# Trunk encoder with a mixture of experts on one core: 2 KB runs for the experts' first weights, norm vectors loaded ahead of weights, the first expert interleaved, and the embedding's second half added on GpSimd

## The chip, the cores and the metric

The kernel runs on 1 core of a Trainium2 chip. The metric is device time in microseconds (us) of one launch, the median of several runs. Engines: PE is TensorE's matmuls, PEld its weight loads, DVE is VectorE, ACT is ScalarE, POOL is GpSimd, SP is SyncE, which here only issues DMAs. All arithmetic is fp32 to the outside; TensorE multiplies in a rounded fp32 format, so that a product is made of three matmuls (below).

## The reference, cut to what matters

Two layers over 512 tokens of width 1024. In each, three mixers read one projection, an output projection follows, then a layer norm (LN1), a mixture of experts beside a gated embedding (PLE), and a second layer norm (LN2).

```python
for i in range(DEPTH):                                   # 2 layers
    u = h @ w_in[i]
    mix = concatenate([hyena(u), diff_attention(u), pool(u)]) @ w_out[i]
    h = layer_norm(DN_ALPHA * h + mix, ln1_g[i], ln1_b[i])          # LN1
    y_moe = hier_moe(h, ...)         # 1 of 4 groups, 2 of its 4 experts, per token
    y_ple = sigmoid(h @ ple_wg[i] + ple_bg[i]) * (p[i] @ ple_wp[i])
    h = layer_norm(DN_ALPHA * h + y_moe + y_ple, ln2_g[i], ln2_b[i])  # LN2

# one expert e of 16, of width 256, on the tokens sent to it:
y_e = (silu(x @ w1[e]) * (x @ w3[e]) * gate) @ w2[e]     # w1, w3: 1024x256, w2: 256x1024
```

## The kernel before, in words

The 512 tokens are four tiles t of 128 rows, `h[t]`, [128, 1024]. **Products.** Every fp32 operand is split into a rounded part and a rest, `whi` by ACT (L224) and `wlo` by DVE (L225); `mm3` then issues three matmuls, hi by hi (L218), hi by lo (L219), lo by hi (L220). Weights thus pass through four stations: a DMA into a slot `raw` issued from SP (L240), the cast, the subtraction, the matmuls.

**Units.** The work with weights is cut into units of up to 512 KB (`add`). `pump` issues loads ahead of use, as far as `ahead_raw` allows and slots of a pool of 34 of 4 KB per partition (`s4`) are free, and the splits as far as `ahead_split` allows; `fill(n)`, `fill_us` and `fill_to` emit the next units' matmuls. So the order of loads is the order of units, and a load waits, on SP's queue, until an older occupant of its slot is done with.

**LN1 and routing.** The layer emits w_out's product (`mo`, summed into h by DVE, L997), and each tile's norm as soon as its four sums are there: `moments` (L362, L364), `rsqrt` on POOL (L305, L308), `ln` (L334 `(h - mean) * gain`, L336 `* rstd + bias`), then its transposes into `hT` (L376). The tiles `gain` (two, 4 KB a partition each) and `bg`, the PLE's bias, are 512 KB DMAs each, broadcast to all partitions. They are issued from SP after `fill_to(i, "last")` under `P_LN`, hence behind the loads that this `fill_to` prefetches. Then come the routing logits `lgT`, `lg`, and a branch on overflow (L1351), which ends a stretch that the scheduler may reorder.

**Experts.** `add_expert_in` makes four units q for expert e: 256 rows of w1 and w3, two DMAs of 256 KB, "(k p) n -> p k n", so that a partition gets from each matrix two rows of 256 numbers (1 KB), 128 rows apart. The moving operand is then [128, 512], w1's and w3's columns side by side; the stationary one is a 128-column piece of `xT`. `gather` fetches an expert's tokens (`xe`), `expert_x` transposes them (`transpose_hl`, `tr`, L376) and splits them into `xT`; `expert_act` (L1293) makes silu and product, and transposes the result (L1298) into `actT`; `add_expert_out` multiplies by w2 into `ye`, which is scattered by a DMA that accumulates in DRAM (`yd`, L1263). `xe` of the next experts is gathered one or two ahead. Expert 0's first products are followed by its `expert_act` at once; from expert 1 on, units of the next stand between.

**PLE and tail.** `add_ple` computes the embedding's halves c = 0 and 1; c = 0 goes to `plz` tiles in `s4` slots, and from there accumulates into `yd` (L1234, POOL queue), c = 1 stays as `z1[t]`. After the last scatter SP loads `h` from `yd` (L1418). `tail_sum` adds for each tile the last two experts' rows (`el`, four matmuls a half, L1441) and z1. For a tile in `ZPE` (tile 1 in layer 0; 1, 2, 3 in layer 1) z1 and h are added on PE by an identity (L1438, L1445) and ACT writes h (L1446); for the others DVE adds the rows to z1 (L1449) and that to h (L1450). LN2 follows (L348, L350).

## Time and profile before

| what | value |
|---|---|
| time, median of 3 | 1038.74 us (1034.38 to 1038.75) |
| profiled execution: its own time | 1037.3 us |
| profiled execution: span, mean granted clock | 1035.5 us, 0.985 |
| busy: PE, PEld, DVE, ACT, POOL | 94%, 77%, 75%, 59%, 16% of the span |
| weights of the experts, 256 loads of 256 KB | 1 KB a run |
| expert stage, layers 0 and 1 | about 334 to 523 and 826 to 1011 us |

The times in the rows are microseconds from the span's start. A matmul's duration is longer than the step from one start to the next, since matmuls are pipelined; its step is read from the chain or from two starts.

### The profile page before, as it was taken

Reading aid. Unit: us, or ns where it says so; the run is one execution under the profiler, and the core shown is the slowest. Engines: PE = TensorE matmul, PEld = TensorE weight load, DVE = VectorE, ACT = ScalarE, POOL = GpSimd, SP = SyncE. Lnnn points to the kernel's source line nnn. Section 1 sums busy time; section 2 is a strip of 40 time slices with the busy share of each in tenths; the row PEclk is TensorE's granted clock in tenths of the full one; section 3 lists DMA queues with packets and bytes.
Section 4 is the critical chain, followed back from the end, with each engine's and each line's share of the span. In section 5 each row is a group of like instructions: output and inputs, shape, how many; then the busy total and the mean of one; then the engine's idle time right before and its main releaser. Section 6 shows DMA issues by size and latency. Waiting matters only on the chain. (4 is left out here: it accounts for less than half of the span.)

```text
span 1035.5 us, 14416 instructions
## 1 busy us (share of the span) xinstructions
PE 969.3 (94%) x4877; PEld 801.8 (77%) x4878; DVE 781.4 (75%) x1305; ACT 613.7 (59%) x1046; POOL 163.6 (16%) x158
## 2 busy tenths in 40 slices
PE   4999999999989999999989999999998999999896
PEld 3887888898867788777768889899776778877673
DVE  7576897777676788887984678847578587888795
ACT  5425464556653768886843336655645286888573
POOL 2101000000121223332112000000003122243111
PEclk9999999999999999999999999999999999999999
DMA  8816121221963999999975321222187399999963
GB/s 267 239 36 143 52 72 53 72 82 63 322 234 106 302 299 318 306 284 307 292 246 137 88 70 53 62 71 72 62 300 248 83 318 294 325 295 306 311 203 156
DMA packets 154922, 195.39 MB, mean 189 GB/s; under 512 B 20232, under 2 KB 123722, under 8 KB 154837
## 3 DMA queue, kind: packets, MB, share of 16 engines
q1 hardware_dynamic: 136405, 159.78, 46.6%
q0 software_dynamic: 18432, 34.57, 13.0%
q8 instruction: 42, 0.69, 0.3%
q14 instruction: 43, 0.35, 0.1%
HBM read 182.85 MB, written 27.26 MB: 203 GB/s over the span
## 5 line engine op out<-in xcount | busy, mean ns | idle before, releaser
L225 DVE TENSOR_TENSOR wlo<-raw,whi 128x1024 fp32r<-128x1024 f32 (+2 forms) x278 | 323.7, 1182 | 62.1 <-ACT whi L224 59.6
L224 ACT CAST whi<-raw 128x1024 fp32r<-128x1024 f32 (+2 forms) x278 | 277.1, 1024 | 24.4 <-DMA raw<-in_ple_wg_dram 6.4
L218 PE MATMUL e<-whi,xT 128*128 128x512 f32 x256 | 106.5, 416 | 2.7 <-ACT xT L224 1.7
L219 PE MATMUL e<-wlo,xT 128*128 128x512 f32 x256 | 103.5, 404 | 0.1
L220 PE MATMUL e<-whi,xT 128*128 128x512 f32 x256 | 101.7, 397 | 0.0
L218 PE MATMUL pj<-whi,hT 128*128 128x384 f32 x256 | 90.1, 353 | 2.3 <-ACT hT L224 1.8
L219 PE MATMUL pj<-wlo,hT 128*128 128x384 f32 x256 | 88.2, 345 | 0.3 <-DVE wlo L225 0.3
L220 PE MATMUL pj<-whi,hT 128*128 128x384 f32 x256 | 87.3, 342 | 0.1
L1263 POOL DMA_INDIRECT yd<-ye,rt_tok x28 | 53.5, 1910 | 202.6 <-ACT actT L224 122.0
L868 ACT ACTIVATE prob<-sc,mx 128x512 f32<-128x512 f32 x64 | 43.8, 688 | 40.4 <-DVE mx L867 38.0
L1257 POOL DMA_INDIRECT xe<-hd,rt_tok x32 | 48.8, 1525 | 90.1 <-PE tr L376 45.6
L308 POOL TENSOR_TENSOR ors<-rs_y,mhalf 128x4 f32<-128x4 f32 x8 | 8.5, 1056 | 336.7 <-DVE rs_y L307 336.7
L218 PEld LDWEIGHTS e<-whi,xT 128*128 128x128 f32 x256 | 48.8, 191 | 12.8 <-ACT xT L224 2.2
L219 PEld LDWEIGHTS e<-wlo,xT 128*128 128x128 f32 x256 | 48.8, 190 | 10.9 <-DVE wlo L225 2.4
L220 PEld LDWEIGHTS e<-whi,xT 128*128 128x128 f32 x256 | 48.7, 190 | 10.1
L218 PE MATMUL mo<-whi,YT 128*128 128x512 f32 x128 | 53.6, 419 | 0.0
L219 PE MATMUL e<-wlo,actT 128*128 128x512 f32 x128 | 51.2, 400 | 2.4 <-DVE wlo L225 2.4
L218 PEld LDWEIGHTS pj<-whi,hT 128*128 128x128 f32 x256 | 49.1, 192 | 4.8 <-ACT hT L224 2.5
L218 PE MATMUL pl<-whi,hT 128*128 128x512 f32 x128 | 50.8, 402 | 1.3 <-ACT whi L224 1.3
L219 PE MATMUL pl<-wlo,hT 128*128 128x512 f32 x128 | 51.4, 402 | 0.5 <-DVE wlo L225 0.5
L218 PE MATMUL e<-whi,actT 128*128 128x512 f32 x128 | 48.2, 398 | 3.8 <-ACT whi L224 2.9
L218 PE MATMUL pj<-hT,whi 128*128 128x512 f32 x128 | 51.1, 403 | 0.0
(344 smaller groups left out, 2310.7 us busy)
## 6 DMA issues: line engine op xcount, KB each, us to landing
raw<-in_moe_w_dram SPq DMA_DIRECT2D x256, 256.0 KB
raw<-in_moe_w_dram SPq DMA_DIRECT2D x64, 512.0 KB
raw<-in_w_in_dram SPq DMA_DIRECT2D x96, 128.0 KB
raw<-in_w_in_dram SPq DMA_DIRECT2D x16, 512.0 KB
raw<-in_ple_wg_dram SPq DMA_DIRECT2D x16, 512.0 KB
raw<-in_w_out_dram SPq DMA_DIRECT2D x14, 512.0 KB
tabi<-c_tabi_dram POOLq DMA_DIRECT2D x8, 516.0 KB, 4.9
tabf<-c_tabf_dram POOLq DMA_DIRECT2D x8, 512.0 KB, 5.6
```

Source lines behind the costliest of these rows:

```text
L218: mm(ps, a[0], b[0], start=start, stop=False)
L219: mm(ps, a[0], b[1], start=False, stop=False)
L220: mm(ps, a[1], b[0], start=False, stop=stop)
L224: self.nc.scalar.copy(hi, src)
L225: self.nc.vector.tensor_sub(lo, src, hi.bitcast(F32))
L308: nc.gpsimd.tensor_tensor(out, y, self.mhalf[:, :n], op=OP.pow)
L868: nc.scalar.activation(p[:, c], o, AF.Exp, bias=mx[:, c:c + 1], accum_out=sm[:, c:c + 1])
L1257: self.nc.gpsimd.indirect_dma_start(out=x, out_offset=None, in_=self.hd[:, :], in_offset=bass.IndirectOffsetOnAxis(ap=tok, axis=0), bounds ...
L1263: self.nc.gpsimd.indirect_dma_start(out=self.yd[:, :], out_offset=bass.IndirectOffsetOnAxis(ap=row, axis=0), in_=y, in_offset=None, bounds ...
```

## The change

Five things are done. (1) `w1` and `w3` are loaded "(p k) n -> p (k n)": a partition gets two neighbouring rows, one run of 2 KB; the two DMAs stay 256 KB each. Row 2p + k of a block now lies in partition p, so the moving operand is two pieces of 256 columns with w1's other row between them, and `xe` is transposed from every second column (`pairs`). (2) `gain` and `bg` are issued ahead of the `P_LN` prefetch. (3) Expert 0's transposes are written a few units earlier, and one unit of expert 1 stands ahead of expert 0's `expert_act`. (4) GpSimd adds z1 to h's second half for each tile; the identity matmul and DVE's add of z1 go, and the halves are taken in the order 0, 1. (5) The first half's `plz` takes one of the two `ye` slots in place of an `s4` slot.

```diff
+    def out4(self):
+        return self.slots.tile([128, 1024], F32, name="ye", tag="ye", bufs=2)
...
-    def transpose_hl(self, src, hi, lo):
+    def transpose_hl(self, src, hi, lo, pairs=False):
...
-                nc.tensor.transpose(ps[:, k * 128:(k + 1) * 128], src[:, c:c + 128], self.ident)
+                x = src[:, c:c + 128]
+                if pairs:
+                    c = half * 512 + k // 2 * 256
+                    x = src[:, c:c + 256].rearrange("p (n k) -> p k n", k=2)[:, k % 2]
+                nc.tensor.transpose(ps[:, k * 128:(k + 1) * 128], x, self.ident)
...
-                    self.plz[t // 2] = self.s4([128, 2, 512], "plz")
+                    self.plz[t // 2] = _view(self.out4(), [128, 2, 512])
...
+        two = lambda t: t.rearrange("p (s n) -> p s n", s=2)
...
-                    self.mm3(st["ps"], [x[:, q * 2 + k] for x in self.xT[e]], [x[:, k] for x in wp],
+                    self.mm3(two(st["ps"]), [x[:, q * 2 + k] for x in self.xT[e]],
+                             [x.rearrange("p s (k n) -> p s k n", k=2)[:, :, k] for x in wp],
...
-            srcs = [((lambda r, s=s: r[:, :, s * 256:(s + 1) * 256]),
-                     A[("moe_w1", "moe_w3")[s]][i, e, q * 256:(q + 1) * 256].rearrange("(k p) n -> p k n", p=128))
+            srcs = [((lambda r, s=s: r[:, s]),
+                     A[("moe_w1", "moe_w3")[s]][i, e, q * 256:(q + 1) * 256].rearrange("(p k) n -> p (k n)", k=2))
...
-        self.transpose_hl(self.xe.pop(e), hi, lo)
+        self.transpose_hl(self.xe.pop(e), hi, lo, pairs=True)
...
+        nc.gpsimd.tensor_tensor(h[:, 512:], h[:, 512:], self.z1[t], op=OP.add)
...
-            for c in (1, 0):
+            for c in (0, 1):
...
-                if zpe and c:
-                    nc.tensor.matmul(ps, self.ident, z, start=True, stop=False)
...
-                if c:
-                    nc.vector.tensor_add(z, z, ps)
-                nc.vector.scalar_tensor_tensor(h[:, cs], h[:, cs], 1.0, z if c else ps, op0=OP.mult, op1=OP.add,
+                nc.vector.scalar_tensor_tensor(h[:, cs], h[:, cs], 1.0, ps, op0=OP.mult, op1=OP.add,
...
+        self.gb = self.gain(A["ln1_g"][i], A["ln1_b"][i])
+        self.bg = self.s4([128, 1024], "bg")
+        nc.sync.dma_start(self.bg, self.row_bcast(A["ple_bg"][i], 1024))
         self.ahead_raw, self.ahead_split = self.P_LN
         self.fill_to(i, "last")
         self.stop = self.marks[i, "pwp"]
-        self.gb = self.gain(A["ln1_g"][i], A["ln1_b"][i])
-        self.bg = self.s4([128, 1024], "bg")
-        nc.sync.dma_start(self.bg, self.row_bcast(A["ple_bg"][i], 1024))
...
         self.overflow(i)
+        while self.pos < self.marks[i, "ple"] - 1:
+            self.fill(1)
+        self.fill_us(2.56)
+        self.expert_x(0)
         self.fill_to(i, "ple")
-        self.expert_x(0)
         for e in range(NE):
-            self.fill(2)
+            self.fill(2 if e != 1 else 1)
...
+            if e == 0:
+                self.fill(1)
             self.expert_act(e)
```

SP's queue around LN1 of layer 1, before and after (a row is a line, an operation, output from input, shape, and how often in a row). Before:

```order
L240 DMA raw<-in_ple_wg_dram 128x2x512 x4
L240 DMA raw<-in_moe_w_dram 128x2x256 x16
L293 DMA gain<-in_ln_g_dram 128x1024
L293 DMA gain<-in_ln_b_dram 128x1024
L1598 DMA bg<-in_ple_bg_dram 128x1024
L240 DMA raw<-in_moe_w_dram 128x1024 x2
```

The same place of the changed kernel:

```order
L244 DMA raw<-in_ple_wg_dram 128x2x512 x2
L297 DMA gain<-in_ln_g_dram 128x1024
L297 DMA gain<-in_ln_b_dram 128x1024
L1601 DMA bg<-in_ple_bg_dram 128x1024
L244 DMA raw<-in_ple_wg_dram 128x2x512 x2
L244 DMA raw<-in_moe_w_dram 128x512 x16
L244 DMA raw<-in_moe_w_dram 128x1024 x2
```

The norm's vectors and the bias move up past two 512 KB loads of ple_wg and sixteen 256 KB loads of experts, whose runs are now 512 numbers.

PE where expert 0's first products end in layer 0; `e_3762` is expert 0's sum, `L1298` (after: `L1309`) its two transposes after silu, `e_3843` the sum of expert 1. Before:

```order
L218 MATMUL e_3762<-whi,xT 128x512
L219 MATMUL e_3762<-wlo,xT 128x512
L220 MATMUL e_3762<-whi,xT 128x512
L1298 MATMUL e_3837<-cst,act 128x128 x2
L218 MATMUL e_3843<-whi,xT 128x512
L219 MATMUL e_3843<-wlo,xT 128x512
```

After, where `e_3837` is the sum of expert 1:

```order
L224 MATMUL e_3837<-whi,xT 128x512
L222 MATMUL e_3837<-whi,xT 128x512
L223 MATMUL e_3837<-wlo,xT 128x512
L1309 MATMUL e_3851<-cst,act 128x128 x2
L224 MATMUL e_3837<-whi,xT 128x512
L384 MATMUL tr<-cst,xe 128x128 x8
```

Eleven matmuls of expert 1 now stand between expert 0's last product and its transposes.

PE at the end of the program, from the last product of the last two experts. Before:

```order
L220 MATMUL e_10888<-whi,actT 128x512
L1441 MATMUL el<-yl,hotT 128x512 x4
L1438 MATMUL el<-plz,cst 128x512
L1441 MATMUL el<-yl,hotT 128x512 x4
L1445 MATMUL el<-h,cst 128x512
L1441 MATMUL el<-yl,hotT 128x512 x4
L1445 MATMUL el<-h,cst 128x512
```

After:

```order
L224 MATMUL e_10888<-whi,actT 128x512
L1450 MATMUL el<-yl,hotT 128x512 x8
L1453 MATMUL el<-h,cst 128x512
L1450 MATMUL el<-yl,hotT 128x512 x4
L1453 MATMUL el<-h,cst 128x512
L1450 MATMUL el<-yl,hotT 128x512 x4
```

The `plz` matmuls are gone from PE. On POOL the four additions stand together, behind the last three scatters and ahead of all four pairs that make LN2's reciprocal deviations. After:

```order
L1271 DMA yd<-ye,rt_tok_8444 512x1024 x3
L1442 TENSOR_TENSOR h<-h,plz 128x512 x4
L309 TENSOR_SCALAR rs_y<-lnvar 128x1
L312 TENSOR_TENSOR lnrs<-rs_y,mhalf 128x1
L309 TENSOR_SCALAR rs_y<-lnvar 128x1
```

Before, L305 and L308 followed the scatters directly.

## Rows read from the trace of the kernel before

**Rows 1.** The page's first part: busy us (share of span) x instructions.

```profile
PE 969.3 (94%) x4877; PEld 801.8 (77%) x4878; DVE 781.4 (75%) x1305; ACT 613.7 (59%) x1046; POOL 163.6 (16%) x158
```

**Rows 2.** Busy time of each engine by stretch, with granted clock, DMA share, GB/s.

```profile
core 0: us, PE busy (x) PEld busy (x) DVE busy (x) ACT busy (x) POOL busy (x), PEclk, DMA share, GB/s
345.00:505.00 160.00, 157.06 (x733) 125.57 (x734) 133.02 (x153) 123.80 (x173) 44.85 (x25) 0.99 0.96 309
835.00:1005.00 170.00, 164.54 (x771) 131.42 (x770) 141.90 (x162) 131.56 (x181) 46.31 (x26) 1.00 0.93 302
526.00:534.00 8.00, 6.01 (x23) 3.79 (x22) 6.41 (x14) 4.60 (x10) 1.11 (x4) 0.91 1.09 354
708.00:709.00 1.00, 1.00 (x7) 1.00 (x6) 0.98 (x2) 0.69 (x1) 0.00 (x0) 1.00 1.04 383
1010.50:1013.50 3.00, 2.67 (x9) 1.28 (x8) 2.10 (x5) 1.37 (x2) 0.00 (x0) 1.00 1.02 401
```

**Rows 3.** Groups of PE instructions, stretch 835 to 1005: busy us, mean ns | idle.

```profile
L376 PE MATMUL tr<-cst,xe 128*128 128x128 f32 x112 | 16.2, 273 | 0.1
L1298 PE MATMUL e<-cst,act 128*128 128x128 f32 x28 | 5.3, 272 | 0.0
```

**Rows 4.** The chain that ended last: start us, us, what.

```profile
924.05 0.23 PE e L219
...
932.17 18.00 DMA raw<-in_moe_w_dram x2
...
981.79 0.87 PE tr L376 x8
```

**Rows 5.** The page's sixth part: loads of the experts' weights, KB each.

```profile
raw<-in_moe_w_dram SPq DMA_DIRECT2D x256, 256.0 KB
```

**Rows 6.** Timeline of PE and ACT, expert 0's transposes in layer 0.

```profile
340.61 2.00 ACT L224 CAST whi<-raw 128x1024 fp32r<-128x1024 f32 x2 [3.07 <-DMA yd<-plz]
342.64 1.28 ACT L1280 ACT_TABLE_LOAD   x1
...
344.83 0.69 PE L1298 MATMUL e<-cst,act 128*128 128x128 f32 x2 [2.26 <-DVE act L1281]
...
346.17 0.63 PE L220 MATMUL e<-whi,xT 128*128 128x512 f32 x1
...
348.29 0.40 PE L219 MATMUL e<-wlo,xT 128*128 128x512 f32 x1
```

**Rows 7.** Timeline of DVE and PE at LN1, layer 0 first, then layer 1.

```profile
281.45 2.48 DVE L334 SCALAR_TENSOR_TENSOR h<-h,lnneg,gain 128x1024 f32<-128x1024 f32 x2 [2.54 <-DMA gain<-in_ln_g_dram]
...
773.08 2.48 DVE L334 SCALAR_TENSOR_TENSOR h<-h,lnneg,gain 128x1024 f32<-128x1024 f32 x2 [2.68 <-DMA gain<-in_ln_g_dram]
...
780.47 1.27 DVE L336 SCALAR_TENSOR_TENSOR h<-h,lnrs,gain 128x1024 f32<-128x1024 f32 x1
...
781.89 1.94 PE L376 MATMUL tr<-cst,h 128*128 128x128 f32 x8 [2.60 <-ACT lnsq L364]
```

**Rows 8.** Timeline of DVE behind the branch, layer 0.

```profile
333.75 0.69 DVE L1208 SCALAR_TENSOR_TENSOR plz<-plz,pwp 128x512 f32<-128x512 f32 x1 [0.32 <-ACT plz L1207]
```

**Rows 9.** The chain in the tail of layer 1.

```profile
1013.34 0.86 PE el L1438 x2
...
1017.76 0.86 PE el L1438 x2
```

**Rows 10.** Timeline of DVE and POOL in the tail of layer 1.

```profile
1013.44 0.68 DVE L1449 TENSOR_TENSOR plz<-plz,el 128x512 f32<-128x512 f32 x1
...
1020.36 0.19 POOL L305 TENSOR_SCALAR rs_y<-lnvar 128x1 f32<-128x1 f32 x1 [2.99 <-ACT lnsq L364]
1024.59 1.28 POOL L305 TENSOR_SCALAR rs_y<-lnvar 128x1 f32<-128x1 f32 x1 [3.41 <-ACT lnsq L364]
```

**Rows 11.** The page's fifth part: POOL's additions and multiplications of four columns.

```profile
L308 POOL TENSOR_TENSOR ors<-rs_y,mhalf 128x4 f32<-128x4 f32 x8 | 8.5, 1056 | 336.7 <-DVE rs_y L307 336.7
```

**Rows 12.** Instructions that read `xe`: duration ns min/median/max, first and last start.

```profile
L376 PEld LDWEIGHTS tr<-cst,xe x256: 137/140/226, 332.1 to 991.7; 128*128 128x128 f32 x128
```

More of the change, by code (lines that the diff above doesn't have):

```diff
@@ L1325, in f @@
                 elif k == 1:
-                    y = self.slots.tile([128, 1024], F32, name="ye", tag="ye", bufs=2)
+                    y = self.out4()
                     for c in range(2):
@@ L1430, in tail_sum @@
         sums = self.sm.tile([128, 2], F32, name="lnsum", bufs=4)
+        nc.gpsimd.tensor_tensor(h[:, 512:], h[:, 512:], self.z1[t], op=OP.add)
         with self.behind():
-            for c in (1, 0):
+            for c in (0, 1):
                 cs = slice(c * 512, (c + 1) * 512)
                 ps = self.ps("el")
-                z = self.z1[t] if c else None
                 zpe = t in self.ZPE[i]
-                if zpe and c:
-                    nc.tensor.matmul(ps, self.ident, z, start=True, stop=False)
                 for e in range(NE - NL, NE):
                     for x in range(2):
-                        nc.tensor.matmul(ps, self.hotT[e][:, t], self.yl[e][x][:, cs],
-                                         start=(e == NE - NL and x == 0 and not (zpe and c)),
+                        nc.tensor.matmul(ps, self.hotT[e][:, t], self.yl[e][x][:, cs], start=(e == NE - NL and x == 0),
                                          stop=(e == NE - 1 and x == 1 and not zpe))
```

## The prediction

> **What bounds the kernel now.** I read the busy shares first: TensorE is busy 94% of the span, the next engine 75% [rows 1]. But a matmul's duration overlaps the next one, so a share of 94% can hide small stops; the step from start to start is the better measure, 0.23 us for a 512-column matmul and 0.87 for eight transposes [rows 4]. So I turned to the windows by stage. In the 160 us of layer 0's expert stage PE has 733 instructions, of them 112 + 28 transposes [rows 2, 3], the same number in both layers. 593 x 0.23 + 140 x 0.109 = 136.4 + 15.3 = 151.7 us of work, hence 8.3 us lost. In layer 1's 170 us: 631 x 0.23 + 15.3 = 160.4, 9.6 us lost. In the same windows the DMA engines are busy 96 and 93%, at 309 and 302 GB/s, while DVE and ACT have a sixth and more of the time free (133.02 and 123.80 of 160) [rows 2]. And the chain of waits, where it leaves PE there, goes into loads of the experts' weights, for two of them 18 us at a stretch [rows 4]. The stage is thus limited by the stream of weights: PE eats what lies in the slots and then waits now and then. The rest of the program is PE, with stops of 1 to 3 us at the seams: LN1, the branch, the first expert, the tails.
>
> **2 KB runs.** Per layer w1 and w3 are 128 loads of 256 KB [rows 5] (the row counts both layers), 33.55 MB. Where the stream was of 1 KB runs alone (w_in, 526 to 534) it moved 354 GB/s with the engines full; of 2 KB runs alone 383 (708 to 709); of longer ones 401 [rows 2]. 33.55 MB take 94.8 us at 354 and 87.6 at 383, so 7.2 us less a layer. That is the value I take; 383 rests on one microsecond, so the bounds are 11.1 us (at 401) and 0. A stage that streams without a gap ends that much sooner if PE has that much to give: layer 0 has 8.3 us and its first stop besides (below), layer 1 has 9.6. So 7.2 each, **14.4 us**, 0 to 20.
>
> The Trainium skill, "DMA: Bandwidth & Descriptors", section "Where 436 GB/s comes from", says that for transfers from HBM the HBM's share of a core, about 358 GB/s, binds; by it 1 KB runs at 354 are at the limit already, and this term would be nothing. The rows at 383 and 401 are against it.
>
> **Two more slots.** The first half of plz leaves two 512 KB slots to weights, 1 MB, at 309 GB/s 3.4 us of lead a layer; it also ends the wait of ACT's cast on the plz transfer, 3.07 us [rows 6]. The lead counts only if the stream is still what limits: I take 0 and keep 3.4 a layer as a bound. The price: expert 0's ye must wait until that transfer has landed, and its two halves run on POOL's queue ahead of the scatter. The cast that waited for it started at 340.61, and ye can't come before the transposes at 344.83 and w2's products [rows 6], so I book nothing.
>
> **First expert.** In layer 0 PE stands 2.26 us before expert 0's transposes (silu's table load of 1.28 and DVE's product lie between), and behind them the matmuls are longer, 0.63 in place of 0.40 up to 348.29 [rows 6]; with steps about twice as long for those 3.5 us, some 1.7 are lost. Eleven matmuls of expert 1 (2.5 us) now stand in the gap. But where the stream of weights limits the stage, time won ahead of it comes back as a wait later; so these 4 us are not booked beside the 7.2, they are what PE can still give (so the bound of the runs' term, 20, is 11.1 of 12 and 9.6 of 9.6, rounded down). Expert 1's transposes and splits must come that much earlier, which the order shows.
>
> **Norm vectors first.** DVE stands idle for gain 2.54 us at 281.45 (layer 0) and 2.68 at 773.08 (layer 1) [rows 7]. In layer 1 tile 1's norm is done only at 781.7, PE waits 2.60 us for it, and then its eight transposes take 1.94 in place of about 1.0 [rows 4, 7]. With gain there at 770.4, L334 and L336 of both tiles need 2.48 + 2 x 1.27 = 5.0 us and end near 775.5, almost 4 before PE is ready (781.89 - 2.60). I take 3.5 us of the 2.60 + 0.9. In layer 0 PE's stops stand further on, behind ACT; I take 1 of 2.54, bounds 0 and 2.5. What is late next: sixteen loads of experts and two of ple_wg wait behind 1.5 MB more, about 4 us at 354 GB/s. Experts are transposed only from 332.1 on [rows 12], 50 us behind layer 0's wait for gain, so nothing is booked. Sum **4.5 us**, 2.5 to 6.
>
> **Behind the branch.** DVE had two plz operations between branch and xT's split, and the second began at 333.75 and took 0.69 [rows 8]. One is left: 0.7 us a layer, **1.4 us**, 0 to 2. The loads stream only from there on, so this counts beside the 7.2.
>
> **GpSimd's addition.** In layer 1's tail PE is the pace: its tiles follow each other by 4.42 us, and the identity product that adds z1 (two records) takes 0.86 of it, in each of three tiles [rows 9]. They go: 2.6 us. In layer 0, and for tile 0 of layer 1, DVE loses an addition of 0.68 [rows 10]; layer 0's first tile has it on the path, 0.6. So 3.2 us. The price is GpSimd's: four additions of 128x512 stand ahead of all four reciprocal deviations of LN2. The trace has no such operation. DVE's takes 0.68; GpSimd's own widest elementwise, four columns, 1.06 with a power in it [rows 10, 11]. And one GpSimd operation of 0.19 us took 1.28 at 1024.59 [rows 10], as long as one of DVE's operations of the norm, 1.27 [rows 7]; I read it as GpSimd held until such a one was done, so either may hold up the other. I take 1.2 us each, near the second row, and 1 us lost over both tails to such meetings. If they begin where DVE now adds z1, at 1013.44, four end near 1018, and only tile 0's deviation comes later for it. Bounds: at 0.68 each nothing lost; at 3.56 each, PE's new step per tile (4.42 - 0.86), they become the pace and 3 us more are gone. Net **2.2 us**, -1 to 3.2.
>
> **Every second column.** The transposes' stationary operand is now read with a stride of two. No row has that. There are 256 such weight loads of 140 ns, and eight transposes step 0.109 us each [rows 4, 12], less than a load's duration, so a longer load is seen at once. Bounds: 0, or twice as long, 256 x 0.14 = 36 us. The moving operand in two pieces keeps 256 neighbours together; I take 0 for both, since the rows that are nearest, the contiguous loads, are all that this trace offers, and keep the 36 as a rival.
>
> The Trainium skill, "SBUF — State Buffer", section "Specifications (TRN2)", says that a read keeps full bandwidth with two hits in each 16-byte line; every second fp32 number has two. By it the stride is free; no run here shows it yet.
>
> **The sum.** 14.4 + 4.5 + 1.4 + 2.2 = 22.5 us, from the profiled execution's 1037.3: 1014.8. The median of the three runs shown is 1.4 us above the profiled one, so 1016.2, rounded to **1016 us**.
>
> **Rivals.**
>
> A. As above. 1016 us, chance 0.52; its own range 1007 (the upper bounds together: 5.6 more from the runs, 1.5, 0.6 and 1.0 from the others) to 1023 (half of the runs' gain).
>
> B. The runs bring little: what limits the stage is the number of loads and the back-and-forth of slots, or a memory rate that 1 KB runs already have; the 309 GB/s in the stage, 45 below 354, show that something beside the run length (the accumulating scatters and the gathers) slows the stream. Then 14.4 is near 0, the time won ahead of the stage is given back, and 4.5 + 1.4 + 2.2 = 8.1 are left: 1030.6 us. For it: 383 stands on one microsecond. Against it: 401 over three. Chance 0.25.
>
> C. The slower side: the strided weight load. Each of 256 transposes gets x ns longer; it decides from 22.5 / 256 = 88 ns on, two thirds of a load. If the load doubles, 1016 + 36 = 1052. For it: the step of a transpose is set by its load. Against: the first eight of an expert could still hide in waits. Chance 0.09.
>
> D. GpSimd's additions become the pace of both tails, 3 us lost where 2.2 were won: 1021 us. For it: 1.28 for a 0.19 operation. Against: the one before it, at 1020.36, was not held [rows 10]. Chance 0.10.
>
> E. The change does little: PE's lost 8 and 10 us are splits and semaphores, not weights, and a seam's wait moves on to the next operation, ACT's logits in LN1 for one. Within 5 us of before, about 1036. Chance 0.04.
>
> **How the numbers follow.** About 0.5% (5.2 us) is what a measurement of this kernel can tell from no change. The likeliest is A. The range reaches from 1007, A's low end, to 1031, B's time, and leaves out C, E and the ends of A and B. Faster by over 0.5%, below 1033.5: A, D and most of B, 0.85. Same: E and a little of B, 0.07. Slower: C less its mild part, 0.08.
>
> **What would show it.** In the windows over the expert stages, GB/s should rise from 309 and 302 by 10 to 20 and PE's lost time fall from 8.3 and 9.6 to some 2 in each; if GB/s rises without PE's waits falling, another engine limits. The waits of L334 on gain should be gone in both layers, and PE's 2.6 us before tile 1's transposes. The 2.26 before expert 0's transposes should be gone. In the tail, tiles should follow each other on PE by 3.56 us in place of 4.42, and L1442's four operations should take near 1.2 us each. The weight loads `tr<-cst,xe` should stay at 140 ns and eight transposes at 0.87. What would make it wrong most: a stream that is no faster, or weight loads that are longer.

## The result, and the profile after

The changed kernel takes 1026.9 us, median of 4 runs (1023.4 to 1028.8), against 1037.14 for the kernel before on the same chip: a ratio of 0.9893 (95% interval 0.985 to 0.9936), 10 us faster. The forecast was 1016, 22.5 us faster; the range held the time. So the direction was right and a little over half of the sum did not come. A second measurement of the same kernel, below, gives 0.9884 (0.9851 to 0.9918).

The page of the changed kernel, span and first part, and one group of the fifth, the cast of all weights.

```profile
span 1027.0 us, 14422 instructions
PE 963.6 (94%) x4869; PEld 803.9 (78%) x4870; DVE 781.7 (76%) x1301; ACT 611.9 (60%) x1046; POOL 174.3 (17%) x166
L228 ACT CAST whi<-raw 128x1024 fp32r<-128x1024 f32 (+2 forms) x278 | 276.7, 1024 | 10.7 <-DVE p L662 4.7
```

The same cast group on the page of the kernel before:

```profile
L224 ACT CAST whi<-raw 128x1024 fp32r<-128x1024 f32 (+2 forms) x278 | 277.1, 1024 | 24.4 <-DMA raw<-in_ple_wg_dram 6.4
```

ACT's idle time ahead of casts fell from 24.4 to 10.7 us, and loads are no longer its largest cause. The runs below share this out: it is 12.0 us with the 2 KB runs alone and 19.6 in the change with 1 KB runs. So most of it is the stream's relief, seen at the first engine behind it. PE lost little less all the same. Busy time by stretch, after:

```profile
345.00:505.00 160.00, 157.09 (x737) 128.17 (x738) 135.70 (x157) 125.63 (x177) 41.07 (x25) 1.00 0.95 318
835.00:1000.00 165.00, 162.40 (x757) 131.84 (x755) 141.87 (x164) 129.34 (x180) 42.80 (x26) 1.00 0.88 295
526.00:534.00 8.00, 5.46 (x17) 4.69 (x18) 5.13 (x11) 4.11 (x10) 1.51 (x4) 0.59 0.76 241
```

In layer 0's window (140 transposes again) 597 x 0.23 + 140 x 0.109 = 152.6, so 7.4 of 160 us are lost where [rows 2, 3] gave 8.3. In layer 1's 165 us (134 transposes) it is 623 x 0.23 + 14.6 = 157.9, 7.1 lost, 9.6 of 170 before. The forecast was 2 in each. (With the steps of the changed kernel itself, 0.231 us and 0.119 for a transpose, it would be 5.4 and 5.1: such a reckoning is good to 2 us.) The stream rose from 309 to 318 GB/s in the first window and fell from 302 to 295 in the second; over the experts stages of the table below it rose from 303 and 309 to 314 and 317, 3 to 4%, where the sum had taken 7.2 of 160 us.

Where the time went is best read stage by stage, from the starts of PE's first or last instruction of a kind in the two traces. LN1 is from w_out's first product (`mo`) to the last logit (`lg`); "first expert" from there to the first w2 product; "experts" from there to the last product of the embedding (`pl`); "end" from there to the last w2 product; "tail" from there to the next layer's first projection, or the span's end.

| stage, us | before, layer 0 | after | before, layer 1 | after |
|---|---|---|---|---|
| LN1 | 159.6 | 158.9 | 154.1 | 151.4 |
| first expert | 46.1 | 42.0 | 43.1 | 41.7 |
| experts | 134.1 | 134.3 | 137.4 | 134.3 |
| end | 35.0 | 34.4 | 32.3 | 32.5 |
| tail | 13.1 | **15.4** | 24.7 | 24.6 |

The gains are LN1 of layer 1 (2.7), the first expert (4.1 and 1.4) and layer 1's experts (3.1). The tails, booked as a gain of 2.2, lost 2.2. The part ahead of `mo`, which the change does not touch, was 1.3 us longer in this execution, so a difference of 1 us in one pair of profiles is not much.

TensorE's granted clock has a part in these differences. For short stretches it falls to the lower of its two levels (1.2 in place of 2.4 GHz), mostly behind a stop of PE, and not at the same places in each profile. The mean granted clock of layer 0's first expert was 0.93 before and 1.00 after, of layer 0's tail 0.90 and 0.80, and of LN1 of layer 1 0.98 and 0.99.

**LN1, layer 1.** DVE after:

```profile
768.84 2.48 DVE L338 SCALAR_TENSOR_TENSOR h<-h,lnneg,gain 128x1024 f32<-128x1024 f32 x2 [0.46 <-DMA raw<-in_moe_w_dram]
771.76 1.28 DVE L340 SCALAR_TENSOR_TENSOR h<-h,lnrs,gain 128x1024 f32<-128x1024 f32 x1 [0.45 <-POOL lnrs L312]
773.78 1.28 DVE L340 SCALAR_TENSOR_TENSOR h<-h,lnrs,gain 128x1024 f32<-128x1024 f32 x1 [0.73 <-POOL lnrs L312]
```

The wait for gain of [rows 7] is gone, and tile 1's norm follows tile 0's at 773.78, where before other work of DVE lay between. Of PE's 2.6 us nothing is left there; a stop of 1.32 has come at the third and fourth tiles:

```profile
790.26 0.31 PE L1040 MATMUL lgT<-hT,gwhl 128*40 128x256 f32 x1 [1.32 <-ACT hT L228]
```

**Layer 0's tail.** GpSimd, DVE and PE after:

```profile
516.25 1.28 POOL L1442 TENSOR_TENSOR h<-h,plz 128x512 f32<-128x512 f32 x1 [8.83 <-DVE wlo L229]
519.91 3.24 POOL L1442 TENSOR_TENSOR h<-h,plz 128x512 f32<-128x512 f32 x2 [0.86 <-DMA h<-yd]
520.15 3.82 DVE L229 TENSOR_TENSOR wlo<-raw,whi 128x768 fp32r<-128x768 f32 x2
528.53 1.97 PE L384 MATMUL tr<-cst,h 128*128 128x128 f32 x8 [4.24 <-DVE h L354]
530.15 3.76 PE L1450 MATMUL el<-yl,hotT 128*128 128x512 f32 x8
```

One addition takes 1.28 us. The third and fourth met two subtractions of DVE, which take 0.95 us each when alone; here the two lasted 3.82 us and the two additions 3.24. They ran nearly one after the other: the pair of DVE takes 1.83 alone and 2 x 1.28 + 1.83 is 4.4, and from 519.91 to 523.97 it is 4.1. DVE's additions to h and tile 0's norm came behind them, PE stood 4.24 us, and then it ran slowly: granted clock 0.59 from 526 to 534, nearer the lower of its two levels (1.2 GHz) than 2.4, and 3.76 us for eight matmuls that take 2.1 in the kernel with a mixed tail below.

**Layer 1's tail.** GpSimd, DVE and PE after:

```profile
1004.37 1.30 POOL L1442 TENSOR_TENSOR h<-h,plz 128x512 f32<-128x512 f32 x1 [0.16 <-DVE yl L1333]
1006.92 1.59 POOL L1442 TENSOR_TENSOR h<-h,plz 128x512 f32<-128x512 f32 x1 [1.25 <-DMA h<-yd]
1008.60 0.19 POOL L309 TENSOR_SCALAR rs_y<-lnvar 128x1 f32<-128x1 f32 x1
1009.47 1.41 DVE L354 SCALAR_TENSOR_TENSOR h<-ln,lnrs,gain 128x512 f32<-128x512 f32 x2 [2.08 <-POOL lnrs L312]
1014.53 1.02 PE L1453 MATMUL el<-h,cst 128*128 128x512 f32 x2
```

PE did its part: its last matmuls start at 1014.53, 12.1 us behind the last w2 product; before it was 14.7 (1025.6). But the span ends 24.6 us behind that product as it did before. The fourth addition waits for the last tile of h, and tile 0's reciprocal deviation, queued behind it on GpSimd, comes late: DVE stands 2.08 us at L354 where it stood 0.8 before. From there the four norms follow each other on DVE, ACT and GpSimd about 4 us apart.

### The profile page after: what moved, and what is told of

Read it like the earlier page. It is cut to its first block, busy times and chain, and to the rows that moved or that the text cites. A ratio compares the mean times of both kernels' runs of the same rounds, so it can differ in the third digit from the quotient of the medians.

```text
span 1027.0 us, 14422 instructions
## 1 busy us (share of the span) xinstructions
PE 963.6 (94%) x4869; PEld 803.9 (78%) x4870; DVE 781.7 (76%) x1301; ACT 611.9 (60%) x1046; POOL 174.3 (17%) x166
## 5 line engine op out<-in xcount | busy, mean ns | idle before, releaser
L228 ACT CAST whi<-raw 128x1024 fp32r<-128x1024 f32 (+2 forms) x278 | 276.7, 1024 | 10.7 <-DVE p L662 4.7
L1271 POOL DMA_INDIRECT yd<-ye,rt_tok x28 | 50.2, 1794 | 195.7 <-ACT ye L1339 102.0
L1265 POOL DMA_INDIRECT xe<-hd,rt_tok x32 | 46.7, 1461 | 95.7 <-PE tr L384 52.2
L222 PEld LDWEIGHTS e<-whi,xT 128*128 128x128 f32 x256 | 48.8, 191 | 12.1 <-ACT whi L228 1.8
L223 PE MATMUL pj<-hT,whi 128*128 128x512 f32 x128 | 51.2, 400 | 0.0
L224 PE MATMUL pj<-hT,wlo 128*128 128x512 f32 x128 | 51.2, 400 | 0.0
L222 PE MATMUL pj<-hT,whi 128*128 128x512 f32 x128 | 51.1, 403 | 0.0
L1339 ACT ACTIVATE ye<-e,rt_gate 128x512 f32<-128x512 f32 x56 | 38.0, 690 | 21.8 <-PE e L224 21.5
```

What stands on the lines that cost most here:

```text
L222: mm(ps, a[0], b[0], start=start, stop=False)
L223: mm(ps, a[0], b[1], start=False, stop=False)
L224: mm(ps, a[1], b[0], start=False, stop=stop)
L228: self.nc.scalar.copy(hi, src)
L1265: self.nc.gpsimd.indirect_dma_start(out=x, out_offset=None, in_=self.hd[:, :], in_offset=bass.IndirectOffsetOnAxis(ap=tok, axis=0), bounds ...
L1271: self.nc.gpsimd.indirect_dma_start(out=self.yd[:, :], out_offset=bass.IndirectOffsetOnAxis(ap=row, axis=0), in_=y, in_offset=None, bounds ...
```

## The experiments

Ratios are against the kernel before on the same chip. The experiments ran on more than one chip, so two of them are compared by their ratios (0.001 is 1 us) rather than by their medians. The stages are those of the table above.

**Theories.** Theory 1: the stream of weights held PE up at a few places only, PE's other lost time belongs to the seams, and GpSimd's additions cost what they save. The rival is the prediction's own reckoning: the stream limits both expert stages throughout.

**The tail of before in the changed kernel.**

```diff
-        nc.gpsimd.tensor_tensor(h[:, 512:], h[:, 512:], self.z1[t], op=OP.add)
...
+                if zpe and c:
+                    nc.tensor.matmul(ps, self.ident, z, start=True, stop=False)
...
+                if c:
+                    nc.vector.tensor_add(z, z, ps)
```

> The changed kernel with the tail of the kernel before (identity matmul and DVE's addition of z1 back, GpSimd adds nothing). Theory 1, from the trace after: GpSimd's four additions hold up the norm behind them; in layer 0's tail PE's stop before tile 0's transposes was 2.35 us and is 4.8, so it should be 2.4 again and the next layer's first projection should come 2 to 2.5 us earlier behind the last expert; in layer 1 the matmuls saved (2.6 us) were eaten by the norm's chain, so nothing is lost there. About 2.5 us faster than the change, near 1024.5. Rival, the prediction's reckoning: the additions are worth 2.2 us net, so 1029.

Measured: 1026.07 us, 0.9888 (0.9854 to 0.9923). Tail of layer 0 12.1 us, of layer 1 24.6. The times can't tell it from the change, so Theory 1's 2.5 us do not show in them; the stages say that the addition is worth nothing in layer 1 and cost 3.3 us in layer 0 in this pair. A part of these 3.3 is the clock: 0.95 over this tail, 0.80 over that of the change.

**1 KB runs in the changed kernel.**

```diff
-                     A[("moe_w1", "moe_w3")[s]][i, e, q * 256:(q + 1) * 256].rearrange("(p k) n -> p (k n)", k=2))
+                     A[("moe_w1", "moe_w3")[s]][i, e, q * 256:(q + 1) * 256].rearrange("(k p) n -> p k n", p=128))
...
-        self.transpose_hl(self.xe.pop(e), hi, lo, pairs=True)
+        self.transpose_hl(self.xe.pop(e), hi, lo)
```

> The changed kernel with the experts' first weights loaded in 1 KB runs again, contiguous transposes, moving operand in one piece; all other parts of the change stay. Theory 1: the stream was what PE waited for only at a few stops (layer 1, near 961 to 967, about 4 us; layer 0, about 1 us), so some 3 to 5 us slower than the change, near 1031, and the first-expert and norm gains stay. Rival, the prediction's: the stream limits both stages, so the time won at the first expert is given back too and the kernel is 14 us slower than the change, 1041 or above before.

Measured: 1026.81 us, 0.9912 (0.9884 to 0.9941). Neither: in time no clear difference (2 to 3 us by the ratios, with intervals that overlap). In the stages, layer 0's experts take 139.9 us, 5.6 more than with 2 KB, and layer 1's 133.8, as with 2 KB; layer 0's tail happened to be 11.5 us.

**2 KB runs alone, in the kernel before** (the diff above the other way round, with the two-piece moving operand).

> The kernel before with the 2 KB runs alone (loads, every second column in the transposes, moving operand in two pieces). Theory 1: 3 to 5 us faster than before, most of it in layer 1 between 960 and 967, where 4 us of stops should go. Rival, the prediction's: 14 us faster, 1023. Second rival: the longer weight loads of the transposes (207 ns in place of 140 in the trace after) cost as much as the runs give, and it is within 1 us of before.

Measured: 1029.92 us, 0.9929 (0.9905 to 0.9952), 7 us: more than Theory 1 had, half of the prediction's. Experts 133.5 and 133.7 us, 4.3 less in sum. Not all of the 7 is the runs' own: in this profile LN1 and the first expert of layer 0 are 2.1 and 1.2 us shorter too, and the part ahead of `mo`, which no edit touches, 2.4, each at a higher granted clock than before.

**Half of the stream.**

```diff
-                    for s in range(2)]
-            self.add(srcs, [2, 512], emit(q))
+                    for s in range(1)]
+            self.add(srcs, [2, 512, 1], emit(q))
...
+                if half:
+                    self.split(hi, lo, raw.to_broadcast([128, 2, 512]))
```

> The changed kernel with half of the experts' first weights loaded: w1 alone, one 256 KB load of 2 KB runs a unit, used for w3 too (the output is that of w3 = w1); casts, subtractions, matmuls and slots are as many as in the change. The stream has 16.8 MB less a layer, some 44 us of it at 383 GB/s. Theory 1: the stream limits little in the change, so the expert stages get at most 1 to 2 us shorter each, near 1024. Rival, the prediction's: the stages are limited by the stream, PE's 6 to 7 us of lost time in each go away with it, near 1014.

Measured: 1022.48 us, 0.986 (0.9828 to 0.9891), about 3 us less than the change by the ratios. Busy time by stretch:

```profile
345.00:505.00 160.00, 158.74 (x757) 131.14 (x755) 138.95 (x161) 129.83 (x182) 38.81 (x26) 1.00 0.79 241
835.00:990.00 155.00, 153.75 (x730) 126.70 (x729) 134.82 (x155) 125.23 (x174) 36.45 (x25) 1.00 0.75 224
```

The DMA engines now have 21 to 25% of the time free, and PE's lost time, reckoned as above (142 and 132 transposes), is 3.1 us in each window (1.0 and 1.2 with the longer steps). So of the 5 to 7 us that the change still loses in a layer some 4 are the stream's and 1 to 3 are not. Both theories were off: Theory 1 had 1 to 2 a layer, the rival 6 to 7. Experts take 131.0 and 131.1 us, 3.2 less than in the change, but LN1 takes 164.5 and 154.7, 5.6 and 3.3 more (in layer 0 PE waits 3.1 us there for DVE's hT), which is why the whole kernel shows less. The run halves the number of loads with the bytes and can't tell the two apart.

**The first expert in the old order.**

```diff
-        while self.pos < self.marks[i, "ple"] - 1:
-            self.fill(1)
-        self.fill_us(2.56)
-        self.expert_x(0)
         self.fill_to(i, "ple")
+        self.expert_x(0)
...
-            self.fill(2 if e != 1 else 1)
+            self.fill(2)
...
-            if e == 0:
-                self.fill(1)
```

> The changed kernel with the first expert as before (expert 0's transposes after all units of the embedding, no unit of expert 1 ahead of its silu). Theory 1: from first product to first w2 product of layer 0 the change took 14.8 us, before 18.9, and the interleaving gave that; undone, 18 to 19 again, layer 1 about 1 us more, the kernel 3 to 5 us slower than the change, near 1031. Rival: the gain came from the plz tiles that left the weight slots (ACT's cast no longer waits 3.07 us for their transfer), so undoing the interleaving costs under 1.5 us.

Measured: 1029.12 us, 0.9923 (0.9897 to 0.995). First expert 43.1 us in layer 0, 1.1 more than the change, and 44.2 in layer 1, 2.5 more. The size fits Theory 1, the place does not: in layer 0 about 3 of the 4.1 us remain without the interleaving.

**Norm vectors late again.**

```diff
-        self.gb = self.gain(A["ln1_g"][i], A["ln1_b"][i])
-        self.bg = self.s4([128, 1024], "bg")
-        nc.sync.dma_start(self.bg, self.row_bcast(A["ple_bg"][i], 1024))
         self.ahead_raw, self.ahead_split = self.P_LN
         self.fill_to(i, "last")
         self.stop = self.marks[i, "pwp"]
+        self.gb = self.gain(A["ln1_g"][i], A["ln1_b"][i])
+        self.bg = self.s4([128, 1024], "bg")
+        nc.sync.dma_start(self.bg, self.row_bcast(A["ple_bg"][i], 1024))
```

> The changed kernel with the norm's vectors and the bias loaded behind the prefetch again. Theory 1 and the prediction agree: DVE waits 2.5 us for gain in each layer, PE 2.6 us and longer transposes in layer 1; about 3.4 us slower than the change (0.7 in layer 0, 2.7 in layer 1), near 1030. Rival: the weights behind the vectors come late in the change, so part of it is given back in the expert stage, and it is within 1.5 us of the change.

Measured: 1026.51 us, 0.9906 (0.9876 to 0.9937), by the ratios 1.3 to 2.3 us slower than the change, with intervals that overlap: the time does not decide between the two. LN1 of layer 1 took 152.1 us, 0.7 more; PE's stop was back, with 2.52 us, and behind it the low clock of the kernel before. The 0.7 understates this, because the change's own profile has a low clock at another place in that stage, in attention, far ahead of the norm. Granted clock (the last figure but two) at tile 1's transposes, before and after, and then in attention, in the change and in the run with the old tail:

```profile
780.00:788.00 8.00, 5.35 (x29) 4.19 (x30) 7.19 (x13) 4.02 (x7) 3.06 (x5) 0.79 0.94 318
776.00:784.00 8.00, 6.97 (x41) 4.96 (x40) 7.68 (x15) 6.15 (x13) 2.88 (x5) 1.00 0.96 348
...
733.00:743.00 10.00, 8.55 (x34) 6.54 (x33) 5.31 (x10) 5.50 (x12) 1.33 (x1) 0.83 0.00 1
732.00:742.00 10.00, 8.55 (x43) 6.69 (x42) 6.03 (x12) 5.73 (x13) 1.33 (x1) 1.00 0.01 3
```

In layer 1 the first expert was 1 us shorter, at a clock of 1.00 in place of 0.96, and the tail took 23.8. The rival's cause, weights that come late, is not what these stages show.

**Every second column alone, in the kernel before.**

```diff
-                     A[("moe_w1", "moe_w3")[s]][i, e, q * 256:(q + 1) * 256].rearrange("(k p) n -> p k n", p=128))
+                     A[("moe_w1", "moe_w3")[s]][i, e, q * 256:(q + 1) * 256].rearrange("(p k) n -> p k n", k=2))
...
-        self.transpose_hl(self.xe.pop(e), hi, lo)
+        self.transpose_hl(self.xe.pop(e), hi, lo, pairs=True)
```

> The kernel before with the experts' transposes reading every second column (and the weights' rows placed to match, still 1 KB pieces). Theory 1: the weight load takes 207 ns in place of 140, but the transposes' steps hide it: in the trace after, transposes in the expert stages took 17.1 and 17.2 us in all, before 17.2 and 17.9; within 1 us of before, 1036. Rival (the prediction's slower side, at the size now seen): 256 x 67 ns = 17 us slower, 1053.

Measured: 1036.17 us, 1.0003 (0.9978 to 1.0029). Instructions that read `xe` in it: duration ns min/median/max.

```profile
L380 PEld LDWEIGHTS tr<-cst,xe x256: 194/207/219, 331.3 to 991.8; 128*128 128x128 f32 x128
L380 PE MATMUL tr<-cst,xe x256: 270/283/357, 331.4 to 992.0; 128*128 128x128 f32 x128
```

The load is 67 ns longer than in [rows 12] and the kernel's time is the same within its interval of 2 to 3 us. Theory 1 held in the time. In the chain eight transposes behind one another take a little longer, 0.95 us here against 0.87 in [rows 4]:

```profile
991.28 0.95 PE tr L380 x8
```

For the 32 groups of eight that is 2.6 us at most, which this interval can't tell from nothing.

**A mixed tail: GpSimd only in the last layer, and not for the last tile.**

```diff
-        nc.gpsimd.tensor_tensor(h[:, 512:], h[:, 512:], self.z1[t], op=OP.add)
+        pool = i == DEPTH - 1 and t < NT - 1
+        if pool:
+            nc.gpsimd.tensor_tensor(h[:, 512:], h[:, 512:], self.z1[t], op=OP.add)
...
```

> The changed kernel where GpSimd adds z1 in the last layer only, for tiles 0, 1 and 2; tile 3 there and layer 0's tiles are added as before. Theory 1: in layer 0 the meeting of GpSimd's additions with DVE's subtractions is gone (tail from the last expert product to the next projection 12 to 13 us in place of 15.4); in layer 1 the fourth addition, which waited for the last tile of h and held up the first reciprocal deviation by 1.25 us, is gone, so 23.4 in place of 24.6. 3 to 4 us faster than the change, near 1023. Rival: the tail is the norm's chain whatever adds z1, so it is within 1 us of the change without GpSimd, 1026.

Measured: 1023.77 us, 0.9878 (0.9849 to 0.9906). Tails 12.1 and 23.6 us, against 15.4 and 24.6 in the change. Layer 0's DVE and PE, and layer 1's GpSimd and DVE:

```profile
520.10 1.83 DVE L229 TENSOR_TENSOR wlo<-raw,whi 128x768 fp32r<-128x768 f32 x2
527.09 1.31 PE L384 MATMUL tr<-cst,h 128*128 128x128 f32 x8 [1.99 <-DVE h L354]
528.16 2.10 PE L1454 MATMUL el<-yl,hotT 128*128 128x512 f32 x8
...
1003.53 0.18 POOL L309 TENSOR_SCALAR rs_y<-lnvar 128x1 f32<-128x1 f32 x1 [2.65 <-ACT lnsq L368]
1004.40 1.41 DVE L354 SCALAR_TENSOR_TENSOR h<-ln,lnrs,gain 128x512 f32<-128x512 f32 x2 [1.12 <-POOL lnrs L312]
```

The two subtractions take 1.83 us again and PE stands 1.99. GpSimd now waits for ACT, not ACT's work for GpSimd. Theory 1 held in both stages, and this is the fastest full kernel of the study by its median, though its interval overlaps that of the change, and by the ratios it is only 1 us faster than the change without GpSimd (0.9888): it is the stages that speak against the rival, not the time.

**The plz slots alone, in the kernel before.**

```diff
-                    self.plz[t // 2] = self.s4([128, 2, 512], "plz")
+                    self.plz[t // 2] = _view(self.out4(), [128, 2, 512])
```

> The kernel before where only the first half's plz tiles take the ye slots. Theory 1, from the run that undid the interleaving: these slots, not the interleaving, gave most of the first expert's gain in layer 0; from the first transposes of xe to the first w2 product 17 to 18 us in place of 20.95, and the stretch from the logits to the first transposes of layer 1 near 25.1 in place of 26.4. Since the runs stay 1 KB, a stop of 3 to 6 us can come back later in a stage: net 0 to 4 us faster than before, 1034. Rival: the interleaving gave it, 20 to 21 us there, and the kernel is within 1 us of before.

Measured: 1033.24 us, 0.9979 (0.9956 to 1.0002). The stretches expected came, 17.6 and 24.9 us, but others grew, as that from the logits to the first transposes of layer 0, 26.8 us (25.2 before). By the stages, first expert 44.4 in layer 0 (46.1 before) and 43.9 in layer 1 (43.1). In layer 1 the first w2 product came 2.4 us later behind the transposes; the interleaving is what takes this back. A stop of 2.26 us stands ahead of expert 0's transposes in layer 0 as in [rows 6], but the transposes behind it are at full speed:

```profile
345.78 0.44 PE L1302 MATMUL e<-cst,act 128*128 128x128 f32 x2 [2.26 <-DVE act L1285]
```

**1 KB runs in the kernel with the mixed tail** (the diff of the 1 KB runs above).

> The kernel with the mixed tail (GpSimd adds in the last layer only, for three tiles) with 1 KB runs. Theory 1: 1 KB kernels had a stop of 2 to 7 us in one or the other expert stage of each profile (134.1 or 140 us in layer 0, 133.8 or 137.4 in layer 1, from the first w2 product to the last of the embedding), 2 KB kernels never (133.5 to 134.3); so 3 to 6 us slower than the same with 2 KB runs, near 1028, with such a stop in the profile. Rival 1, the prediction: 14 us, 1038. Rival 2, from the times of the two kernels with the full change: no difference, 1024.

Measured: 1029.69 us, 0.9919 (0.989 to 0.9948); its 2 KB counterpart had 0.9878, so 4 us more by the ratios and 5.9 by the medians, with 142.5 us for layer 0's experts. PE's long waits there, the granted clock from 470 to 485, and ACT's waits:

```profile
472.79 0.81 PE L222 MATMUL e<-whi,actT 128*128 128x512 f32 x2 [1.81 <-ACT whi L228]
477.73 1.22 PE L222 MATMUL pl<-whi,hT 128*128 128x512 f32 x2 [1.18 <-ACT whi L228]
...
470.00:485.00 15.00, 11.53 (x32) 7.64 (x31) 8.70 (x10) 8.86 (x12) 1.85 (x1) 0.66 0.92 295
...
ACT whi L228 <- DMA raw<-in_ple_wg_dram: 3.6, 1, 3.6
ACT whi L228 <- DMA raw<-in_moe_w_dram: 2.8, 2, 2.7
```

The two stops are 3 us in sum, the stage is 8 us longer than with 2 KB runs (134.3): the rest goes with the clock, 0.66 over these 15 us.

**The change again**, unaltered.

> The changed kernel unaltered, for a second profile. Theory 1: the layer 0 tail is a meeting of GpSimd's additions with DVE's subtractions, whose cost hangs on when h's tiles arrive: from the last expert product to the next projection 11.5 us without a meeting, up to 15.4 with one; no stop in the expert stages (134 us in each from first w2 product to the embedding's last). 1024 to 1027. Rival: the 15.4 is fixed by the order of the work and comes again to within 0.5 us.

Measured: 1025.79 us, 0.9884 (0.9851 to 0.9918). Experts 134.3 and 134.3 us again. Tail of layer 0 14.2 us (granted clock 0.86), not 15.4: the rival falls. DVE's pair and GpSimd's:

```profile
519.41 3.25 POOL L1442 TENSOR_TENSOR h<-h,plz 128x512 f32<-128x512 f32 x2 [1.60 <-DMA h<-yd]
520.14 3.33 DVE L229 TENSOR_TENSOR wlo<-raw,whi 128x768 fp32r<-128x768 f32 x2
```

**Norm vectors early alone, in the kernel before** (the diff of the vectors above the other way round).

> The kernel before with the norm's vectors and the bias loaded ahead of the prefetch, and nothing else. Theory 1: PE's stop of 2.7 us before tile 1's transposes in layer 1 goes, and a stop of 1 us comes in its place; w_out's first product to the last logit in layer 1 near 150.5 in place of 153 to 154, layer 0 unchanged; 2 to 3 us faster than before, 1034. Rival: weights that wait behind the vectors give it back in the expert stage, and it is within 1 us of before.

Measured: 1032.26 us, 0.9948 (0.9926 to 0.9971), 4 to 5 us. The profiled execution was a long one, 1041.5 us, 9 above the median (span 1039.6): LN1 of layer 1 151.6 as expected, but both expert stages had a stop, 139.5 and 140.5 us.

## Why the prediction was half right

Experts' stage and the tails in every profile but that of the half stream, us:

| kernel | runs | experts, layers 0 / 1 | GpSimd adds in layer 0 | tails, layers 0 / 1 | granted clock, layer 0's tail |
|---|---|---|---|---|---|
| before | 1 KB | 134.1 / 137.4 | no | 13.1 / 24.7 | 0.90 |
| stride alone | 1 KB | 139.6 / 133.8 | no | 13.3 / 24.6 | 0.87 |
| plz slots alone | 1 KB | 135.3 / 133.3 | no | 11.9 / 24.6 | 1.00 |
| vectors alone | 1 KB | 139.5 / 140.5 | no | 13.2 / 24.7 | 0.89 |
| change, 1 KB | 1 KB | 139.9 / 133.8 | yes | 11.5 / 25.8 | 1.00 |
| mixed tail, 1 KB | 1 KB | 142.5 / 133.9 | no | 12.1 / 23.6 | 0.96 |
| 2 KB alone | 2 KB | 133.5 / 133.7 | no | 13.2 / 24.7 | 0.89 |
| change, twice | 2 KB | 134.3 / 134.3, 134.3 / 134.3 | yes | 15.4 / 24.6, 14.2 / 24.6 | 0.80, 0.86 |
| old tail | 2 KB | 134.3 / 134.4 | no | 12.1 / 24.6 | 0.95 |
| first expert plain | 2 KB | 133.7 / 133.4 | yes | 13.9 / 25.2 | 0.87 |
| vectors late | 2 KB | 134.2 / 134.2 | yes | 14.2 / 23.8 | 0.88 |
| mixed tail | 2 KB | 134.3 / 134.2 | no | 12.1 / 23.6 | 0.96 |

**2 KB runs: the mechanism right, the term mis-sized.** The prediction booked 14.4 us, because "The stage is thus limited by the stream of weights". The table shows what the runs do: with 1 KB one of the two stages, or both, is 3 to 8 us longer in five of six profiles. There PE's units wait for ACT and ACT for a load, in stops of 1 to 4 us, and in five of these six long stages the granted clock is below 1.00 as well (0.96 to 0.99). With 2 KB none of seven profiles has such a stage, each takes 133.4 to 134.4 us, and its clock is 1.00. Summed over both layers that is 273.9 on average against 268.2, 6 us. The profiled executions with 1 KB were on average 2.4 us above their kernels' medians and those with 2 KB 0.2, so some 2 of the 6 are chance; the ratios give 2 to 3 (full change), 4 (mixed tail) and 7 us (alone). The step that failed is the count of what PE had to give. 8.3 and 9.6 us were lost, but 1 to 3 of them stay in each window with half the stream, and some 4 more with 2 KB runs. The stream rose by 3 to 4%, not by the 8% between 354 and 383 GB/s: the stretch of one microsecond was no measure for a stage in which other transfers run too. So rival B's reason was partly true.

The rule cited from the Trainium skill, "DMA: Bandwidth & Descriptors", section "Where 436 GB/s comes from", would have 1 KB runs at the limit already and no gain; the table is against that here, though no run here has a second core on the same memory.

**First expert: not booked, and it came.** The argument was that time won ahead of a limiting stream comes back as a wait. With 2 KB runs it stayed won (42.0, then 134.3 for the experts). With 1 KB runs the experts of layer 0 took 139.9 and 142.5 us behind a first expert of 40.8 and 40.6, but 139.5 and 139.6 also behind one of 46.0 and 44.9 (vectors alone, stride alone), and layer 1's took 133.8 and 133.9 behind 40.9 and 40.7: no run shows that what was won comes back. Of the edits, the interleaving gives 1.1 and 2.5 us. The rest in layer 0 goes for the most part with the granted clock of this stage: in the old order 46.1 and 46.0 us at 0.93, 44.9 twice at 0.96, with the plz slots alone 44.4 at 0.96, with the slots and 2 KB runs 43.1 at 1.00; in the new order with 2 KB runs 41.5 to 42.1, all at 1.00. So the plz slots give about 0.5 at like clock. The clock was below 1.00 in this stage in five of six profiles with the old order and in none of seven with the new and the whole stream.

So the range held the time in part by luck: 5.5 of the 10 us came from a stage that the sum had at nothing, and made up for terms that brought less or went the other way.

**Norm vectors: right in layer 1, with 2.7 in place of 3.5; nothing clear in layer 0**, where 1 was booked: but for the half stream, the stage took 157.5 to 160.5 with the vectors early or late. In layer 1 all five profiles with late vectors have a stop of 2.5 to 2.6 us before tile 1's transposes and the low clock behind it, and none of eight with early vectors has either. A stop of 1.3 at the third and fourth tiles, not foreseen, took the difference. The stage took 149.9 to 150.0 us in four early profiles and 151.3 to 151.6 in the four with the low clock in attention; late ones took 152.1 to 153.4 without that and 154.0 and 154.1 with it. Like for like the vectors are thus worth 2.2 to 3.4 us there. With the vectors late the kernel took the same time within its interval, alone early they gave 3 to 8 us by theirs.

**Behind the branch.** Booked 1.4 in two halves; measured 0 in layer 0 and 1.3 in layer 1, and there, as it seems, from another edit: the stretch from the last logit to the first transposes of layer 1 falls from 26.4 to 25.1 us without the interleaving too, and to 24.9 with the plz slots alone. It scatters, though: 25.9 with the vectors alone.

**GpSimd's addition: wrong.** Booked at 2.2 us of gain, it is worth nothing in layer 1 on average. "In layer 1's tail PE is the pace" failed: PE's tiles did come 3.56 us apart, yet the chain of four norms on DVE, ACT and GpSimd, 4 us a tile, was as long, and took over at once. It was visible before: the last matmul ended near 1026, and the span ran to 1035.5. In all fourteen profiles, additions or not, the span ends 18.4 to 19.0 us behind tile 0's first reciprocal operation on GpSimd. The additions only move the start of that operation: 4.9 to 7.4 us behind the last w2 product with them, according to when the tiles of h land, and 5.6 to 5.9 without. Late vectors, with four additions done early, had 23.8, as short as the mixed tail.

The price of an addition (1.28, booked 1.2) was right. The meeting with DVE, booked at 1 us over both tails, costs up to 2 us of DVE in layer 0: 1.83 us for DVE's pair without additions, 2.06 to 3.82 with them, the more the later the third addition starts. What follows from it is mixed with the clock. Layer 0's tail, before, after, with the plz slots alone and in the change with 1 KB runs:

```profile
522.20:535.30 13.10, 10.79 (x37) 6.51 (x36) 11.07 (x20) 7.14 (x14) 1.50 (x4) 0.90 1.04 349
518.30:533.70 15.40, 10.81 (x34) 7.26 (x33) 12.26 (x19) 7.14 (x14) 5.50 (x7) 0.80 0.93 306
...
522.00:533.90 11.90, 9.57 (x37) 5.68 (x36) 9.96 (x18) 7.15 (x14) 1.20 (x4) 1.00 1.05 354
524.80:536.30 11.50, 8.68 (x35) 5.30 (x34) 9.56 (x17) 7.13 (x14) 3.41 (x6) 1.00 1.09 351
```

Without additions the tail takes 11.9 to 12.1 us at a clock of 0.95 to 1.00 and 13.1 to 13.3 at 0.87 to 0.90; with them 11.5 at 1.00, 13.9 to 14.2 at 0.86 to 0.88 and 15.4 at 0.80. At like clock they are worth 0.4 us won to about 1 lost; the rest of the 3.3 between the change and its old tail goes with the clock. It fell at each of the four stops of 3.3 to 4.2 us that the meetings made before tile 0's transposes, and at four of ten stops of 2.0 to 2.5. Rival D had the mechanism, as the pace of tails; the mixed tail shows that it is the order on GpSimd's queue and the meeting, not the pace.

**Every second column: right, for another reason.** Taken as free; the load is 67 ns longer. The Trainium skill, "SBUF — State Buffer", section "Specifications (TRN2)", asks for two hits in each line for full bandwidth and adds that each cross to a new line pays a penalty. A stride of two has the two hits but crosses twice as often; the prediction drew on the first half alone, and the weight load's duration (207 against 140 ns) fits the second. The time agrees because the step from one transpose to the next grows by 10 ns only (0.95 against 0.87 us for eight). Rival C's break-even of 88 ns was for loads that show; these hardly do.

What stays open: why the stop with 1 KB runs falls now in one layer and now in the other, and why the granted clock falls behind one stop and not behind another of the same length.

## What to carry to other kernels

Lost time of the bounding engine is not all the bounding stream's: before booking it, sort its stops by what they recur with, or halve the stream once and see what is left. Compare the stages of two profiles only beside their granted clocks: a stretch at the lower level was worth over 1 us here, as much as the smaller terms of the sum. An edit that frees an engine in a tail is worth the distance to the next chain only; read how far the span goes on behind that engine's last instruction. Work moved to an idle engine stands in that engine's queue: put nothing that waits for a late transfer ahead of a small operation on the critical chain.

## What the runs showed of the hardware

- A GpSimd addition and a DVE subtraction, each with two operands in SBUF, run nearly one after the other: two of 1.28 and two of 0.95 us that met took 4.1 us together (519.91 to 523.97), little less than the 4.4 of one after the other; DVE's pair lasted 3.82 in place of 1.83.
- A weight load of 128x128 fp32 from every second column takes 207 ns, from neighbouring columns 140; eight transposes behind one another took 0.95 us in place of 0.87 (the kernels' times differ by 0.03%).
- A stop of 4.24 us of PE ahead of layer 0's last transposes went with a granted clock of 0.59 over 8 us; stops of 1.98 (before, 0.90 over the tail) and 1.99 us (plz slots alone, 1.00 over the tail) at the same place show that the same stop can come with either level.
